# Loading 17 of 32 row pairs, and storing 11, as single 64 KB runs in a streaming softmax-gradient kernel

## The chip, the cores and the metric

The kernel runs on one core of a Trainium2 chip. The metric is the time of one execution on the device, in microseconds (us). A time with a range is the median of three to nine runs. The profiler adds nothing that matters: a profiled execution of the kernel before took 1248.14 us, the unprofiled ones 1248.03 to 1248.1 us.

## The reference, cut to what matters

```python
# logits: 8 x 1024 x 8192 float32, labels: 8 x 1024
logits_max = np.max(logits, axis=-1, keepdims=True)
exp_logits = np.exp(logits - logits_max)
softmax = exp_logits / np.sum(exp_logits, axis=-1, keepdims=True)
# one_hot has 1.0 at the label of each row
return (softmax - one_hot).astype(np.float32)
```

268 MB are read and 268 MB written, with a little arithmetic between: a streaming problem.

## The kernel before: the parts that matter

The 8192 rows are cut into 64 tiles of 128 rows (one per partition, 32 KB each). Tiles 2b and 2b+1 form block b: partition p holds rows 2p and 2p+1 of the block, which are neighbours in memory. Six slots of the on-chip buffer X hold one tile each. Here "row" means such a row tile, 4 MB.

```python
x_b = x_nv.rearrange("(b p j) v -> b p j v", p=P, j=G)   # G = 2
X = const.tile([P, SLOTS, V], fp32)                      # SLOTS = 6
...
def load(t, n):        # issued by SyncE; waits until the slot's old row is stored
    free = [stored[u - SLOTS] for u in range(t, t + n) if u - SLOTS in stored]
    w = run(nc.sync, free, got[t % SLOTS], "dma_start", out=sbuf(t, n), in_=hbm(x_b, t, n))
def store(t, n):       # issued by ScalarE; waits for the last arithmetic on the row
    w = run(nc.scalar, [finished[t + n - 1]], put[t % SLOTS], "dma_start", ...)
...
for t in range(T):     # cut to its order
    # ScalarE: x = exp(x - max), sum      VectorE: 1 / sum
    load(t + 1, 1)     # VectorE: maximum of row t + 1
    store(t - 1, 1)
    # ScalarE: x * 1/sum                  VectorE: subtract the one-hot row
```

## Time and profile before

| | before |
|---|---|
| time, median of 3 (range) | 1248.08 us (1248.03 to 1248.1) |
| bytes moved, mean rate | 536.98 MB, 431 GB/s |
| VectorE (DVE) busy, ScalarE (ACT) busy | 90%, 74% |
| last load landed, last store issued | 1199.2 us, 1229.6 us |

These lines of the page give the busy share of the DMA engines and the rate in 40 equal slices of the span, then the packets (here 16384 records of 32 KB, one for each run of bytes, and 2064 of 4 bytes, 16 for each of the 129 transfers, which I take for the semaphore writes), then the transfers with their median time from issue to landing.

```profile
DMA  9999999999999999999999999999999999999998
GB/s 406 418 430 433 435 434 430 433 435 433 431 434 434 433 431 434 434 432 431 434 435 432 431 434 434 431 433 434 435 431 433 433 434 432 432 433 435 431 432 385
DMA packets 18484, 536.98 MB, mean 431 GB/s; under 512 B 2064, under 2 KB 2064, under 8 KB 2096
...
X<-in_logits_dram SPq DMA_DIRECT2D x64, 4096.0 KB, 24.2
out_dram<-X ACTq DMA_DIRECT2D x64, 4096.0 KB, 55.1
```

The DMA is full in every slice but the last, and all from the third to the last but one read 430 to 435 GB/s. (A slice counts a packet whole where it starts, so single slices of the page after the change read up to 442.) A store needs 55 us from issue to landing and one is issued every 19.4 us, so two to three stores stand in their queue. The next lines are the view by stretches (start and end, length, busy time of PE, PEld, DVE, ACT and POOL with instruction counts, clock, DMA share, GB/s).

```profile
60.00:300.00 240.00, 0.00 (x0) 0.00 (x0) 240.00 (x43) 198.35 (x43) 0.00 (x0) 1.00 1.00 433
300.00:600.00 300.00, 0.00 (x0) 0.00 (x0) 269.80 (x48) 223.74 (x48) 0.00 (x0) 1.00 1.00 433
600.00:900.00 300.00, 0.00 (x0) 0.00 (x0) 270.78 (x47) 221.40 (x47) 0.00 (x0) 1.00 1.00 433
900.00:1050.00 150.00, 0.00 (x0) 0.00 (x0) 134.15 (x24) 111.95 (x24) 0.00 (x0) 1.00 1.00 433
```

The rate is 433 GB/s throughout. The end of the kernel in the timeline (start, length, engine, operation, tiles, and in brackets the idle time before it and what ended that):

```profile
1199.19 8.69 DVE L64 TENSOR_REDUCE m<-X 128x1 f32<-128x8192 f32 x1 [1.94 <-DMA X<-in_logits_dram]
...
1216.57 0.34 ACTq L64 DMA_DIRECT2D out_dram<-X  x1
...
1229.60 0.34 ACTq L64 DMA_DIRECT2D out_dram<-X  x1
```

The last load lands at 1199.2 us, and the last store is issued 30 us later. The stores that still stand in the queue fill those 30 us (426 to 439 GB/s in every 5 us from 1200 to 1230).

### The profile page before, as it was taken

Reading aid. Unit: us, or ns where it says so; the run is one execution under the profiler, and the core shown is the slowest. Engines: PE = TensorE matmul, PEld = TensorE weight load, DVE = VectorE, ACT = ScalarE, POOL = GpSimd, SP = SyncE. Lnnn points to the kernel's source line nnn. Section 1 sums busy time; section 2 is a strip of 40 time slices with the busy share of each in tenths; the row PEclk is TensorE's granted clock in tenths of the full one; section 3 lists DMA queues with packets and bytes.
Section 4 is the critical chain, followed back from the end, with each engine's and each line's share of the span. In section 5 each row is a group of like instructions: output and inputs, shape, how many; then the busy total and the mean of one; then the engine's idle time right before and its main releaser. Section 6 shows DMA issues by size and latency. Waiting matters only on the chain.

```text
span 1246.4 us, 592 instructions
## 1 busy us (share of the span) xinstructions
PE 0.4 (0%) x2; PEld 0.3 (0%) x2; DVE 1121.3 (90%) x196; ACT 919.0 (74%) x194; POOL 7.4 (1%) x7
## 2 busy tenths in 40 slices
PE   0000000000000000000000000000000000000000
PEld 0000000000000000000000000000000000000000
DVE  5999999999988989889898898998988989889893
ACT  3888888888767777677767777777777777677772
POOL 2000000000000000000000000000000000000000
DMA  9999999999999999999999999999999999999998
GB/s 406 418 430 433 435 434 430 433 435 433 431 434 434 433 431 434 434 432 431 434 435 432 431 434 434 431 433 434 435 431 433 433 434 432 432 433 435 431 432 385
DMA packets 18484, 536.98 MB, mean 431 GB/s; under 512 B 2064, under 2 KB 2064, under 8 KB 2096
## 3 DMA queue, kind: packets, MB, share of 16 engines
q1 hardware_dynamic: 9216, 268.44, 50.0%
q10 hardware_dynamic: 9264, 268.51, 49.9%
q14 instruction: 4, 0.03, 0.0%
HBM read 268.50 MB, written 268.44 MB: 431 GB/s over the span
## 4 chain that ended last, share of the span: by engine, by line
another core or an unknown queue 69%; DVE 21%; DMA 6%; SPq 1%; ACT 1%; DVEq 0%; issue 0%; PE 0%; ACTq 0%
DVE m L64 10%; DVE X L64 10%; DMA out_dram<-X 4%; DMA X<-in_logits_dram 2%; SPq L64 1%; ACT X L64 1%; DVE iota L64 0%; DVEq L52 0%; DMA lab_raw<-in_labels_dram 0%; DVE lab_f L64 0%; DVE r L64 0%; PE iota L64 0%; ACTq L64 0%; DVE lab L64 0%
## 5 line engine op out<-in xcount | busy, mean ns | idle before, releaser
L64 DVE TENSOR_REDUCE m<-X 128x1 f32<-128x8192 f32 x64 | 555.6, 8681 | 91.4 <-DMA X<-in_logits_dram 91.4
L64 ACT ACTIVATE X<-X,m 128x8192 f32<-128x8192 f32 x64 | 455.8, 7122 | 187.9 <-DVE m L64 187.9
L64 DVE SCALAR_TENSOR_TENSOR X<-iota,lab,X 128x8192 f32<-128x8192 int16 (+1 forms) x65 | 559.6, 8610 | 4.1 <-ACT X L64 4.1
L64 ACT ACTIVATE X<-X,r 128x8192 f32<-128x8192 f32 (+1 forms) x65 | 456.0, 7016 | 116.0 <-DVE r L64 116.0
L64 DVE RECIPROCAL r<-s 128x1 f32<-128x1 f32 x64 | 9.8, 153 | 7.3 <-ACT X L64 7.3
L64 ACT ACTIVATION_READ_ACCUMULATOR X<-X,m 128x1 f32 x64 | 11.9, 186 | 0.0
L64 DVE CAST lab_f<-lab_raw 32x256 f32<-32x256 int32 x1 | 3.5, 3526 | 4.9 <-DMA lab_raw<-in_labels_dram 4.9
L64 POOL IOTA X<- 128x8192 int16 x1 | 6.9, 6943 | 0.0
L64 DVE TENSOR_SCALAR iota<-X 128x4096 int32<-128x4096 int32 x1 | 4.4, 4427 | 0.1
L64 ACT ACT_TABLE_LOAD x1 | 1.3, 1283 | 1.4 <-SPq L52 1.4
L64 DVE COPY lab<-iota 128x64 f32<-128x64 f32 x1 | 0.2, 224 | 0.5 <-PE iota L64 0.5
L64 PE MATMUL iota<-ident,lab_f 32*128 32x32 f32 x2 | 0.4, 300 | 8.5 <-DVE lab_f L64 8.5
L64 PEld LDWEIGHTS iota<-ident,lab_f 32*128 32x128 f32 x2 | 0.3, 196 | 8.4 <-DVE lab_f L64 8.4
L64 POOL TENSOR_SCALAR_AFFINE_SELECT ident<-ident 32x32 f32<-32x32 f32 x1 | 0.2, 202 | 0.1
L64 POOL MEMSET ident<- 32x32 f32 x1 | 0.1, 114 | 0.5 <-SPq L52 0.5
L176 POOL MEMSET const-bfloat16-1.0<- 128x1 bf16 x1 | 0.1, 106 | 0.0
L176 POOL MEMSET const-uint8-127<- 128x1 uint8 x1 | 0.1, 106 | 0.0
L176 POOL MEMSET const-float32-0.0<- 128x1 f32 x1 | 0.1, 103 | 0.2 <-issue 0.2
L176 POOL MEMSET const-float32-1.0<- 128x1 f32 x1 | 0.1, 103 | 0.0
## 6 DMA issues: line engine op xcount, KB each, us to landing
X<-in_logits_dram SPq DMA_DIRECT2D x64, 4096.0 KB, 24.2
out_dram<-X ACTq DMA_DIRECT2D x64, 4096.0 KB, 55.1
lab_raw<-in_labels_dram ACTq DMA_DIRECT2D x1, 64.0 KB, 3.9
```

Of the source, the lines that this page charges most:

```text
L64: instruction = getattr(engine, method)(**operands)
L176: nc = _bacc.Bacc("TRN2", target_bir_lowering=False, num_devices=1)
```

## The change

The intent is to spend less on each run of bytes: where a block's two rows are loaded or stored together, each partition moves one run of 64 KB instead of two of 32 KB. Loads are paired in 17 of 32 blocks, stores in 11, the ends stay row by row, and the last load comes in two halves so that its maximum can start early.

```diff
+PAIRED_LOADS = (1, 2, 4, 5, 7, 8, 10, 11, 13, 14, 16, 17, 19, 20, 22, 23, 26)
+PAIRED_STORES = (4, 7, 10, 13, 16, 19, 22, 24, 26, 29, 30)
-        def load(t, n):
+        def load(t):
+            if t % G and t // G in PAIRED_LOADS:
+                return
+            n = G if t // G in PAIRED_LOADS else 1
             free = [stored[u - SLOTS] for u in range(t, t + n) if u - SLOTS in stored]
+            cols = halves if t == T - 1 else [slice(None)]
+            # one dma_start for each of cols
-        def store(t, n):
+        def store(t):
+            if t // G in PAIRED_STORES:
+                if t % G == 0:
+                    return            # the first row waits for the second
+                t -= t % G
+            n = G if t // G in PAIRED_STORES else 1
             w = run(nc.scalar, [finished[t + n - 1]], ...)
 ... (row_max of the last row: two halves and a minimum of the two)
```

More of the change, by code (lines that the diff above doesn't have):

```diff
@@ L47 @@
     m, s, r = (const.tile([P, T], fp32, name=n) for n in ("m", "s", "r"))
+    m_halves = const.tile([P, 2], fp32)
     iota = psum.tile([P, V], i16)
@@ L53 @@
         sem = tc.alloc_semaphore
-        got = [sem(f"got{i}") for i in range(SLOTS)]
+        got = [sem(f"got{i}") for i in range(SLOTS + 1)]
         put = [sem(f"put{i}") for i in range(SLOTS)]
@@ L100 @@
         loaded, stored, w_max, finished = {}, {-1: w_iota}, [], []
+        halves = [slice(0, V // 2), slice(V // 2, V)]
         def hbm(rows, t, n):
@@ L107, in sbuf @@
             return X[:, t % SLOTS : t % SLOTS + n, :]
-        def load(t, n):
+        def load(t):
+            if t % G and t // G in PAIRED_LOADS:
+                return
+            n = G if t // G in PAIRED_LOADS else 1
             free = [stored[u - SLOTS] for u in range(t, t + n) if u - SLOTS in stored]
-            w = run(nc.sync, free, got[t % SLOTS], "dma_start", out=sbuf(t, n), in_=hbm(x_b, t, n))
-            loaded.update(dict.fromkeys(range(t, t + n), w))
-        def store(t, n):
+            to, of = sbuf(t, n), hbm(x_b, t, n)
+            cols = halves if t == T - 1 else [slice(None)]
+            w = [
+                run(nc.sync, free, got[q], "dma_start", out=to[:, :, c], in_=of[:, :, c])
+                for q, c in zip((t % SLOTS, SLOTS), cols)
+            ]
+            loaded.update(dict.fromkeys(range(t, t + n), w))
+        def store(t):
[4 more added lines that the diff above has]
+            n = G if t // G in PAIRED_STORES else 1
             w = run(
@@ L121, in row_max @@
         def row_max(t):
-            w_max.append(run(
-                nc.vector, [loaded[t]], dve, "tensor_reduce",
-                out=m[:, t : t + 1], in_=X[:, t % SLOTS, :], axis=mybir.AxisListType.X, op=Alu.max, negate=True,
-            ))
-        load(0, 1)
+            x, to = X[:, t % SLOTS, :], m[:, t : t + 1]
+            parts = [(x, to)] if len(loaded[t]) == 1 else [(x[:, c], m_halves[:, i : i + 1]) for i, c in enumerate(halves)]
+            for arrived, (part, extreme) in zip(loaded[t], parts):
+                w = run(
+                    nc.vector, [arrived], dve, "tensor_reduce",
+                    out=extreme, in_=part, axis=mybir.AxisListType.X, op=Alu.max, negate=True,
+                )
+            if len(parts) == 2:
+                w = run(
+                    nc.vector, [w], dve, "tensor_tensor",
+                    out=to, in0=m_halves[:, 0:1], in1=m_halves[:, 1:2], op=Alu.min,
+                )
+            w_max.append(w)
+        load(0)
         row_max(0)
@@ L137 @@
             if t + 1 < T:
-                load(t + 1, 1)
+                load(t + 1)
                 row_max(t + 1)
             if t > 0:
-                store(t - 1, 1)
-            n = 1 if t + 1 < T else 2
-            cols = [slice(i * V // n, (i + 1) * V // n) for i in range(n)]
+                store(t - 1)
+            cols = [slice(0, V)] if t + 1 < T else halves
             scaled = [
@@ L158 @@
             finished.append(w)
-        store(T - 1, 1)
+        store(T - 1)
         for w in dict.fromkeys(stored[t] for t in range(T - SLOTS, T)):
```

## The prediction

> **What bounds the kernel now.** The DMA engines. The page shows 536.98 MB in a span of 1246.4 us, 431 GB/s, DMA at nine or more tenths in 39 of 40 slices; DVE is busy 90%, ACT 74%. The stretch views show DMA full from 2 to 1240 us. In steady state one row tile (4 MB in, 4 MB out) takes 19.35 us: the spacing of landings of successive stores; at the end, with stores alone, 9.675 us. [...] the trace's slices reach 435. [...]
>
> **What the change removes.** 17 pairs of loads and 11 pairs of stores become one transfer each. If a 64 KB run is one descriptor, each pair saves eight descriptors and one semaphore write on each engine[...]. A gain of 2% (25 us) is out of reach, since the bytes stay.
>
> **What it moves.** A paired load waits until both slots are stored, and its first row is usable only when both have landed; a paired store waits for its second row, about 19 us more. Slots have slack for it: a store takes 55 us from issue to landing (page, DMA issues), mostly queueing. Stepping the schedule through with the trace's durations (maximum 8.69, exponential with its read 7.3, scaling 7.12, last step 8.74, issue to first packet 1.4 us), the queues never run dry in the middle; pairing everything would idle the DMA by 90 us. DVE has 19.35 - 17.6 = 1.8 us of slack per row.
>
> The danger is the end. Before, DMA stays full to 1240 us: the last load lands at 1199.2, the last store is issued at 1229.6, while the store before it lands only at 1235.4. After, a paired store of rows 60 and 61 is issued later and the last load depends on how the engines share. [...] If a 64 KB packet counts as one turn, the late loads wait behind the 64 KB stores (the last one, in 16 KB halves of a row's 32 KB, gets a fifth of the engine), and DMA idles some 5 to 8 us near 1205 us: total about 1253. If shares stay equal by bytes, or the runs are cut into 32 KB, the end idles about 1 to 1.5 us: total 1247.5 to 1249.5. The list looks tuned, so I lean to the second.
>
> **Prediction.** 1248 us; 8 in 10 between 1245 and 1253. Faster by over 2%: 1%; within 2%: 97%; slower by over 2%: 2%.
>
> **What would show it.** Packets fall from 18484 by about 4000 if 64 KB goes as one. Steady spacing per pair of rows 38.7 us[...]. DMA slices stay at 9 to the last two or three, where one may dip. DVE waits for loads become fewer and longer. The last load's second half lands at 1190 to 1202.
>
> **What would make it wrong.** A 64 KB run handled faster or slower than two of 32 KB; a dry queue in the middle, repeated every three blocks; the packet turns starving the last loads more than I assume.

The sum came to 1248 us: the 1248.1 us before, less a small saving on packets, plus the 1 to 1.5 us of idle time at the end in the favoured branch (5 to 8 us in the other, hence its 1253). The eight and the one on each engine are in the trace before: a 4 MB transfer leaves 128 records of 32 KB and 16 of 4 bytes on 16 engines. The stepped schedule and the idle times are estimates from the durations listed there, and the two branches for how the engines share were suppositions.

## The result, and the profile after

| | before | after |
|---|---|---|
| time, median of 6 (range) | 1248.07 us (1247.91 to 1248.1) | 1260.38 us (1256.36 to 1262.96) |
| ratio | | 1.0096 (95%: 1.0076 to 1.0116) |

A ratio is the mean time of one kernel's fast runs over that of the other's of the same rounds, so it is not quite the ratio of the medians quoted. Executions over 1.5% slower than the fastest of the same kernel are left out of the means. The change costs about 1%, outside the predicted 1245 to 1253 us, and the time now varies by 6.6 us where it had varied by 0.2.

The same lines of the page, after:

```profile
DMA  9999999999999999999999999999999999999998
GB/s 402 426 433 441 426 439 425 434 434 432 430 427 442 421 422 433 432 422 434 423 434 414 437 427 428 415 428 438 420 413 433 417 426 432 434 433 432 438 428 367
DMA packets 14597, 536.98 MB, mean 427 GB/s; under 512 B 1633, under 2 KB 1633, under 8 KB 1665
...
out_dram<-X ACTq DMA_DIRECT2D x42, 4096.0 KB, 32.3
X<-in_logits_dram SPq DMA_DIRECT2D x29, 4096.0 KB, 26.6
X<-in_logits_dram SPq DMA_DIRECT2D x2, 2048.0 KB, 39.7
X<-in_logits_dram SPq DMA_DIRECT2D x17, 33.3
out_dram<-X ACTq DMA_DIRECT2D x11, 28.5
```

There are 3887 fewer packets, so a 64 KB run is one packet (the trace has 3584 records of 64 KB, 128 for each of the 28 paired transfers). The DMA share has not moved at all. The rate has: slices of 413 to 423 GB/s now come at intervals. A store lands 28 to 32 us after issue instead of 55: its queue has lost its backlog. By stretches:

```profile
60.00:300.00 240.00, 0.00 (x0) 0.00 (x0) 223.81 (x40) 184.82 (x40) 0.00 (x0) 1.00 1.00 433
300.00:600.00 300.00, 0.00 (x0) 0.00 (x0) 270.56 (x48) 223.59 (x48) 0.00 (x0) 1.00 1.00 429
600.00:900.00 300.00, 0.00 (x0) 0.00 (x0) 257.93 (x46) 217.78 (x46) 0.00 (x0) 1.00 1.00 428
900.00:1050.00 150.00, 0.00 (x0) 0.00 (x0) 133.35 (x23) 106.06 (x23) 0.00 (x0) 1.00 1.00 422
```

The engines are counted as busy all the time (share 1.00), but they deliver 1 to 2.5% less in the middle. 300 us at 429 instead of 433 are 2.8 us lost, the next 300 us at 428 are 3.5, and 150 us at 422 are 3.8: together about 10 us of the 11.6 by which the profiled run (1259.74 us) is longer. The loss is in the middle, and it is no idle time.

**Where it happens.** The timeline around one of the slow places:

```profile
414.00 8.74 DVE L68 SCALAR_TENSOR_TENSOR X<-iota,lab,X 128x8192 f32<-128x8192 int16 x1
...
426.64 8.69 DVE L68 TENSOR_REDUCE m<-X 128x1 f32<-128x8192 f32 x1 [3.82 <-DMA X<-in_logits_dram]
435.24 8.74 DVE L68 SCALAR_TENSOR_TENSOR X<-iota,lab,X 128x8192 f32<-128x8192 int16 x1
...
444.02 0.34 ACTq L68 DMA_DIRECT2D out_dram<-X  x1
```

Row 20 is finished at 422.7 us (414.00 + 8.74), but its store waits for row 21, finished at 444.0. Between 405.5 and 444.0 us no store is issued. The store before has landed by 438.1 us, and the trace's packet records show no store packet on any engine from 436.6 to 448.3 us: the store queue is dry and the engines run loads alone. When the paired store then arrives, this is what one of the 16 engines does (packet records of the trace; one engine's packets are told apart by each starting where the one before ends):

```
load   32 KB  443.12 -> 444.33   1.21 us
load   32 KB  444.33 -> 445.55   1.21
load   32 KB  445.54 -> 447.32   1.78   stretched
load   32 KB  447.32 -> 449.67   2.35   stretched
store  64 KB  449.66 -> 452.08   2.42
load   32 KB  452.08 -> 453.29   1.21
store  64 KB  453.29 -> 455.71   2.42
```

From about 445.4 us, 1.4 us after the store's issue (the first load's first packet started 1.4 us after its issue, at 2.38 us in the trace before), the last load packets before it take up to twice their time. An undisturbed packet takes 611 ns for 16 KB, 1213 for 32 KB and 2418 for 64 KB, the medians of the trace. I call what a packet takes beyond its size's median, where it is over 30 ns, "stretch", and sum it over all packets and divide by 16 engines. It is 1.3 us before and 12.0 us after. After the first 60 us there are ten stretches of time of over 10 us without a store packet. The table gives them with the packet stretch around the end of each (from 9 us before it to 6 us after):

| store queue dry, us | 203-214 | 319-331 | 437-448 | 554-565 | 672-683 | 790-802 | 908-920 | 977-989 | 1058-1074 | 1173-1184 |
|---|---|---|---|---|---|---|---|---|---|---|
| stretch, us | 0.2 | 0.8 | 1.0 | 1.3 | 1.7 | 1.5 | 1.7 | 1.5 | 0 | 0 |

Together 9.6 us. So the first theory, R: pairing a store makes it wait, the store queue runs dry, and when it starts again beside a running load the engines lose about a microsecond, some eight times. (The load queue runs dry as well, 18 times for 9 to 19 us after the first 60 us, with at most 0.1 us of stretch around the end of each. So it takes more than a dry queue to cost time.)

### The profile page after: what moved, and what is told of

The parts are those of the page before. It is cut to its first block, busy times and chain, and to the rows that moved or that the text cites. A ratio compares the mean times of both kernels' runs of the same rounds, so it can differ in the third digit from the quotient of the medians.

```text
span 1258.0 us, 575 instructions
## 1 busy us (share of the span) xinstructions
PE 0.4 (0%) x2; PEld 0.3 (0%) x2; DVE 1118.7 (89%) x198; ACT 919.0 (73%) x194; POOL 7.4 (1%) x7
## 4 chain that ended last, share of the span: by engine, by line
DVE 50%; DMA 48%; ACT 1%; DVEq 0%; issue 0%; PE 0%; ACTq 0%; SPq 0%
DMA X<-in_logits_dram 25%; DVE X L68 24%; DVE m L68 24%; DMA out_dram<-X 22%; ACT X L68 1%; DVE m_halves L68 1%; DVE iota L68 0%; DVEq L56 0%; DMA lab_raw<-in_labels_dram 0%; DVE lab_f L68 0%; DVE r L68 0%; PE iota L68 0%; ACTq L68 0%; DVE lab L68 0%; ACTq L214 0%
## 5 line engine op out<-in xcount | busy, mean ns | idle before, releaser
L68 DVE TENSOR_REDUCE m<-X 128x1 f32<-128x8192 f32 x63 | 546.4, 8673 | 110.1 <-DMA X<-in_logits_dram 110.1
L68 DVE TENSOR_REDUCE m_halves<-X 128x1 f32<-128x4096 f32 x2 | 8.7, 4406 | 0.0
```

The lines of the kernel that those rows point to most:

```text
L68: instruction = getattr(engine, method)(**operands)
```

## The experiments

All results were correct. The kernels are variants of the changed one; "before" was run beside each set and had medians of 1248.09 to 1248.14 us. The diffs are shortened.

### First set: which part costs

Loads alone.

```diff
-PAIRED_STORES = (4, 7, 10, 13, 16, 19, 22, 24, 26, 29, 30)
+PAIRED_STORES = ()
```

> All 17 paired loads and the split last load stay, every store goes row by row. Theory R (the loss comes when the store queue runs dry and starts again beside a running load, about 1.2 us a time, nine times, and about 3 us at the end): no store waits for its partner, the store queue never runs dry after the first 50 us, so 1246.5 to 1248.5 us and load packets stretched by no more than before (1.7 us per engine in sum). Rival S (64 KB load packets are themselves slower, or starve the stores by taking two turns' worth): half or more of the 12 us stays, 1253 us or more.

Measured: 1251.47 us (1249.99 to 1252.1), ratio 1.0029. No dry stretch after the first 52 us, stretch 2.0 us (before's, given as 1.7 in the expectation, is 1.3 by the definition above). The view by stretches is back to the kernel before:

```profile
300.00:600.00 300.00, 0.00 (x0) 0.00 (x0) 271.24 (x48) 224.27 (x48) 0.00 (x0) 1.00 1.00 433
600.00:900.00 300.00, 0.00 (x0) 0.00 (x0) 264.69 (x47) 218.30 (x47) 0.00 (x0) 1.00 1.00 434
900.00:1050.00 150.00, 0.00 (x0) 0.00 (x0) 137.28 (x25) 113.38 (x25) 0.00 (x0) 1.00 1.00 433
```

Paired loads cost nothing in the middle; rival S falls. About 3 us more than expected remain, taken up in the second set.

Stores alone: `PAIRED_LOADS = ()` and the last load whole.

> The 11 paired stores stay, every load goes row by row. Theory R: paired stores still wait for their second row and the store queue runs dry, some 5 to 8 times, the end also idles; 1252 to 1262 us. Rival S (the paired loads cost it): back to 1247 to 1249 us.

Measured: 1266.27 us (1261.84 to 1271.82), ratio 1.0148: above both ranges and worse than the whole change. Rival S falls again, but R does not explain it all. The store queue runs dry nine times with at most 0.4 us of stretch each; the 12.4 us of stretch lie elsewhere, half of them on store packets, and the engines drift apart (one transfer's landings on the 16 engines are spread over up to 29 us, where before it was 2.3). 11 us more idle time than before lie at the end: the last load lands only at 1225.3 us, with few stores left to fill the time.

The wait without the 64 KB store run: a "paired" store is issued as two 32 KB-run transfers, both when the second row is done.

```diff
-            w = run(nc.scalar, [finished[t + n - 1]], put[t % SLOTS], "dma_start",
-                    out=hbm(o_b, t, n), in_=sbuf(t, n))
+            for u in range(t, t + n):
+                stored[u] = run(nc.scalar, [finished[t + n - 1]], put[u % SLOTS], "dma_start",
+                                out=hbm(o_b, u, 1), in_=sbuf(u, 1))
```

> As after, but a paired store is issued as two transfers of 32 KB runs, both only when the second row is finished: the wait stays, the 64 KB store run goes. Theory R: the dry stretches of the store queue stay in the middle (about eight of 11 to 12 us from the last packet to the next), so about 1 us each is still lost; with a shorter end than after: 1254 to 1260 us. Rival U (the large packet of the restarting store is what stalls the engine, not the restart): 1247 to 1250 us, with stretched load packets at or below 3 us per engine in sum.

Measured: 1259.37 us (1257.4 to 1265.27), ratio 1.0098, as the whole change; stretch 8.1 us in the profiled run. It differs from the loads-alone kernel only in when eleven stores are issued. So the wait costs, and a long store packet is not needed; rival U falls.

Seven pairs, no pairs at the end: `PAIRED_STORES = (4, 7, 10, 13, 16, 19, 22)`.

> As after, but the last four paired stores (blocks 24, 26, 29, 30) go row by row. Theory R: the seven or eight dry stretches up to 920 us stay and cost 8 to 10 us, the end is full again: 1255 to 1258 us. Rival T (all of the loss is the end, the stretched packets cost nothing on balance): 1246 to 1249 us.

Measured: 1260.15 us (1254.92 to 1262.51), ratio 1.0091. Seven dry stretches, stretch 12.6 us. The list's odd tail is not the cause; rival T falls.

### Second set: the end, the dose, the size

Loads alone with the last load whole (`cols = [slice(None)]`).

> Paired loads only, and the last load in one piece again. The theory for the 2 to 4 us that the loads-only kernel still lost: the two 16 KB halves of the last load get a third of the engine against 32 KB stores, so it landed late and the last store was issued at 1235.7 instead of 1229.6 us. Then this kernel is back at 1246.5 to 1248.5 us, with the last store issued by 1231 us. Rival (paired loads cost something in the middle): it stays at 1250 to 1252 us.

Measured: 1247.93 us (1247.46 to 1248.47) against 1248.09, ratio 0.9999 (0.9986 to 1.0011). So the halves, not the pairs, cost the loads-alone kernel its 3 us (without the pairs they cost 1.2, as the run after next shows).

Three pairs: `PAIRED_STORES = (7, 13, 19)`, the rest as changed.

> As after with paired stores in blocks 7, 13 and 19 alone (seven of them and no tail gave 1254.9 to 1262.5 us, none gave 1250.0 to 1252.1 us). Theory R: three dry stretches of the store queue, near 320, 550 and 790 us, each 1 to 1.8 us of stretched load packets: 1253 to 1257 us. Rival (a paired store costs only through a lasting drift that any one of them sets off): as much as with seven, 1258 us or more; or nothing, 1250 to 1252 us.

Measured: 1255.11 us (1253.0 to 1256.6), ratio 1.0051. The dose fits: none 1251.5, three 1255.1, seven 1260.2 us. In the profiled run (1256.6) the account is less tidy, though: 4.4 us of stretch and 4.7 us of idle time at the end beyond before's.

The halves alone: no pairs.

> The kernel before with the last load in halves and nothing else. If packets take turns whatever their size, the second half lands later than the whole did (1199.2 us) and the last store is issued later: 1248.5 to 1251 us. If turns go by bytes, 1247 to 1248.3 us.

Measured: 1249.27 us (1249.17 to 1251.15), ratio 1.0013. The end of its timeline:

```profile
1208.86 4.42 DVE L68 TENSOR_REDUCE m_halves<-X 128x1 f32<-128x4096 f32 x1 [7.32 <-DMA X<-in_logits_dram]
...
1235.19 0.34 ACTq L68 DMA_DIRECT2D out_dram<-X  x1
```

The second half lands at 1208.8 us where the whole load had landed at 1199.2, and the last store is issued at 1235.2 instead of 1229.6. Between 1199 and 1206 us its packet records hold 72 load packets of 16 KB and 61 store packets of 32 KB: packets of the two sizes are about as many, so the loads got 37% of the bytes there. I read this as turns of about one packet for each queue, whatever its size. The halving meant to start the maximum early made it late.

All of the change with runs of 32 KB: the two slots of a pair are put three slots apart, so a pair is still one transfer with the same waits.

```diff
-            return X[:, t % SLOTS : t % SLOTS + n, :]
+            i = t % SLOTS
+            at = i // G + (i % G) * (SLOTS // G)
+            return X[:, at : at + (n - 1) * (SLOTS // G) + 1 : SLOTS // G, :] if n > 1 else X[:, at : at + 1, :]
```

> All of the change, but the two slots of a pair lie apart in the on-chip buffer, so a pair is still one transfer with the same waits and every run is 32 KB (about 18,500 packets again). Theory R in its plain form (any restart of a dry store queue costs about 1 us, the size of a packet does not matter): stepping it through gives some 16 dry stretches, so 1258 us or more. Rival V (the loss needs 64 KB packets, as turns that favour one queue or as long packets): 1248 to 1251 us, most of it at the end.

Measured: 1256.58 us (1254.94 to 1257.64), ratio 1.0067, a little under the range of plain R and far above that of V. The cost does not need 64 KB packets. But the place is another one: seventeen dry stretches of the store queue ended with 0.3 us of stretch or less each, and most of the 9.1 us came in bursts of 0.3 to 1.6 us within 20 us after the load queue had been dry for about 20 us and was issued to again. R in its plain form, every restart costs a microsecond, is wrong.

### Third set: paired stores with and without a dry queue

Every second paired load only, `PAIRED_LOADS = (1, 4, 7, 10, 13, 16, 19, 22)`, the last load whole, three or seven paired stores; the three-store control with all paired loads; and the seven-store kernel with the buffer's pairs of slots turned by one place.

> Paired stores in blocks 7, 13 and 19 as in the run with three of them, but only every second of the paired loads (blocks 1, 4, ... 22) and the last load whole. Stepped through with the rule that each packet is one turn, the stores then keep a backlog and their queue never runs dry. Theory R: no dry stretch, no stretched packets, 1247 to 1249 us. Rival W (a paired store costs about 1.2 us wherever it stands): 1251 to 1253 us.

Measured: 1254.02 us (1253.13 to 1254.72), ratio 1.0047, above both ranges. The premise failed: the store queue did run dry, three times for 6 to 9 us, with 0, 1.8 and 1.7 us of stretch.

> The control of the run above: all paired loads, paired stores in blocks 7, 13 and 19, the last load whole. Theory R: three dry stretches of 11 to 12 us, 1 to 1.6 us of stretching each: 1250.5 to 1253.5 us. Rival W: the same time as the run above.

Measured: 1250.66 us (1249.71 to 1251.39), ratio 1.0022. Three dry stretches as expected, but only 0.0, 0.4 and 0.2 us of stretch at them: the time lies in R's range, and not for R's reason. Neither theory foresaw that this control would be the faster of the two.

> The run with seven paired stores and no paired tail, with the three pairs of slots in the on-chip buffer turned by one place, so that the restarting stores read another part of it. If the cost of a restart is a matter of timing between queues: 1255 to 1262 us as before. If it hangs on which part of the buffer the store reads (restarts near 1070 and 1180 us in the changed kernel, which read the last two slots, stretched nothing): 1250 to 1253 us.

Measured: 1259.84 us (1256.94 to 1262.07), ratio 1.0092. Which part of the buffer the store reads does not decide.

> Seven paired stores as in the run that had no paired tail, with every second paired load only and the last load whole. Stepped through there is no dry stretch in the middle, and about 3 us of idle time at the end. Theory R: 1248 to 1252 us against 1255 to 1262 us. Rival W (each paired store costs where it stands): 1255 us or more.

Measured: 1270.18 us (1268.94 to 1271.52), ratio 1.0177. The premise failed here too (seven dry stretches), and the end was far worse than stepped through: the last load landed at 1227.0 us, with 13.4 us more idle time than before. My reading, not tested: paired stores take 64 KB turns from single-row loads; the loads fall behind, and at the end no backlog of stores is left.

### Fourth set: feed the queue

The third set had left open whether paired stores cost as such. Here the first half of a pair's first row is stored as soon as that row is finished, and the other one and a half rows when the second is: 48 KB runs remain, the store queue is fed.

```diff
             if t // G in PAIRED_STORES:
-                if t % G == 0:
-                    return
+                lo, hi = (0, V // 2) if t % G == 0 else (V // 2, G * V)
+                # store columns lo to hi of the block when row t is finished
```

> All paired loads, the last load whole, and in the seven blocks with paired stores the first half of the first row is stored as soon as that row is finished (16 KB runs); the other one and a half rows go as 48 KB runs when the second row is finished. The large runs stay, but the store queue is fed again before it runs dry. Theory R: no dry stretch of 8 us or more in the middle, stretching within 2 us of before, 1246.5 to 1249.5 us. Rival W (large store runs, or waiting for the second row, cost where they stand): 1252 us or more.

Measured: 1248.07 us (1247.85 to 1248.74) against 1248.13, ratio 1.0000 (0.9986 to 1.0015).

> The control of the run above: the same seven blocks stored as true pairs, all paired loads, the last load whole. Theory R: seven dry stretches, 1252 to 1258 us, with 4 to 10 us of stretching. Rival W: within 1.5 us of the run above.

Measured: 1257.55 us (1255.26 to 1259.17), ratio 1.0069. First the fed kernel by stretches, then the control:

```profile
300.00:600.00 300.00, 0.00 (x0) 0.00 (x0) 271.04 (x48) 224.07 (x48) 0.00 (x0) 1.00 1.00 433
600.00:900.00 300.00, 0.00 (x0) 0.00 (x0) 263.47 (x47) 217.07 (x47) 0.00 (x0) 1.00 1.00 433
900.00:1050.00 150.00, 0.00 (x0) 0.00 (x0) 137.79 (x24) 114.25 (x24) 0.00 (x0) 1.00 1.00 434
```

```profile
300.00:600.00 300.00, 0.00 (x0) 0.00 (x0) 268.24 (x48) 221.26 (x48) 0.00 (x0) 1.00 1.00 427
600.00:900.00 300.00, 0.00 (x0) 0.00 (x0) 258.75 (x45) 217.60 (x46) 0.00 (x0) 1.00 1.00 425
900.00:1050.00 150.00, 0.00 (x0) 0.00 (x0) 135.61 (x23) 109.22 (x23) 0.00 (x0) 1.00 1.00 430
```

The fed kernel has no dry stretch after the first 52 us and 2.2 us of stretch; the control has seven, and 12.2 us. The two differ in nothing but how those seven stores are cut and when their first part is issued. Feeding the queue gives back all of the 9.4 us. So withholding the first row's store is shown to be the cause of the loss, twice: here, and in the held kernel against the loads-alone kernel (1259.4 against 1251.5 us), which differ in the time of issue alone. How the wait turns into lost time is less certain: 9.1 of the control's 12.2 us of stretch stand around its seven restarts of the dry store queue, but restarts after dry stretches as long cost next to nothing in the kernel with 32 KB runs.

### The account

For the profiled run of each kernel: the time beyond before's 1248.14 us, and from its packet records the change in stretch, in idle time of the engines up to the last packet, and in undisturbed packet time (medians times counts), each per engine.

| kernel | median, us | profiled: longer by | stretch | idle | packet time | sum |
|---|---|---|---|---|---|---|
| after | 1260.4 | +11.6 | +10.7 | +2.1 | -1.7 | +11.1 |
| loads alone | 1251.5 | +1.8 | +0.7 | +1.8 | -1.0 | +1.6 |
| loads alone, last whole | 1247.9 | -0.2 | +0.9 | -0.1 | -1.1 | -0.3 |
| stores alone | 1266.3 | +21.7 | +11.1 | +11.1 | -0.7 | +21.5 |
| held, 32 KB stores | 1259.4 | +9.7 | +6.8 | +3.6 | -1.0 | +9.4 |
| seven pairs, last whole | 1257.6 | +11.0 | +10.9 | +1.5 | -1.5 | +10.8 |
| the same, fed | 1248.1 | -0.1 | +0.9 | +0.0 | -1.0 | -0.1 |
| all with 32 KB runs | 1256.6 | +9.4 | +7.8 | +1.5 | +0.1 | +9.4 |
| half the loads, seven pairs | 1270.2 | +23.4 | +10.7 | +13.4 | -1.0 | +23.1 |

In these kernels stretch, idle time and saved packet time account for the difference to within half a microsecond or so. Busy and idle time fill the span, so the sum has to come out; the table says where the time went, not why.

## Why the prediction was wrong, point by point

- **The bound: right.** The DMA engines bound the kernel before and after (share 1.00 in every stretch above), and no variant won 2% (best ratio 0.9999).
- **The saving: right in kind.** A 64 KB run is one packet (3887 fewer; "about 4000" was predicted). It takes 2418 ns against twice 1213, so 8 ns are saved per run: 1.7 us in the account.
- **The sharing rule: the wrong branch was favoured.** The prediction named both and leaned to equal shares by bytes or runs cut to 32 KB. The traces show turns of about one packet, whatever its size: 64 KB store, 32 KB load, 64 KB store on the engine above; between 1190 and 1206 us of the changed kernel 74 load packets of 16 KB and 5 of 32 KB beside 92 store packets of 64 KB, so the loads got 19% of the bytes; and the half loads that came late in the halves-alone run (72 packets of 16 KB beside 61 of 32 KB). Every run was a packet record of its own: 256 of 16 KB, 9088 of 32 KB and 3584 of 64 KB make up the 536.87 MB of loads and stores. The list that "looks tuned" was no evidence.
- **The end, in that branch: mis-sized.** It foresaw 5 to 8 us of idle time near 1205 us. Measured were 2.1 us more idle time in all. The last half load landed at 1216.9 us, not at 1190 to 1202.
- **The step that failed: "the queues never run dry in the middle".** Its next words cost a dry queue as idle time of the engines alone, and these always had work: while the store queue was dry, loads ran. But the store queue alone was dry ten times for 11 to 16 us, because a paired store withholds a finished row for about 21 us and the backlog that would have bridged this is gone: a store took 55 us from issue to landing before, about 30 after. (It took 33.0 us with the loads paired alone, 33 to 35 with the stores paired alone and 23 to 25 with 32 KB runs throughout, so the 64 KB turns of one queue are not what empties it.) Around eight of the ten returns of the stores, running load packets were stretched, 9.6 us in all. The steady spacing, predicted as 38.7 us per pair of rows (less a small saving), became 39.2 (588.4 us for the 15 pairs between the dry stretches at 319.2 and 907.6 us). The sum of the prediction had no such term, though it had listed "a dry queue in the middle, repeated every three blocks" among what would make it wrong. The held kernel and the fed kernel, each with its control, show that the withheld row is the cause.
- **"DMA slices stay at 9": right, and useless.** A stretched packet counts as busy: the share is 1.00 at 422 GB/s as at 433. GB/s by slice or stretch would have been the thing to name.
- **VectorE's waits for loads: right.** Fewer and longer: 19 waits of 110.1 us in all, where 47 had taken 91.4 us (the view of waits). VectorE still has idle time to spare.

Open: why one restart costs 1.7 us and another nothing. Two restarts of the changed kernel, at 1074 and 1184 us, were free; so were nearly all store restarts of the kernel with 32 KB runs, which paid at load restarts. The length of the dry stretch, the size of the arriving packet, the part of the buffer read and the direction each fail to sort them; the load queue of the loads-alone kernel restarted 16 times after 9 to 12 us without packets, with 0.1 us of stretch or less each. Also open: the spread of 6.6 us between executions, since each kernel has one profile, and the drifting apart of the engines in the stores-alone run.

No variant beats the kernel before. Paired loads with the last load whole and the fed stores tie with it (ratios 0.9999 and 1.0000): the 1 us saved on packets (1.1 and 1.0 in the account) is met by as much stretch (0.9 and 0.9), within what these runs can tell.

## What to carry to other kernels

When the DMA engines are the limit, do not hold back a store that is ready in order to merge it with the next one without measuring: the wait can cost more than the merge saves, even though the engines never idle (here 9.4 us against less than 2). Where a run is one packet and each queue gets about one packet per turn, as here, run lengths set the shares (16 KB load runs beside 32 KB store runs got 37% of the bytes, and the last half load landed at 1208.8 us where the whole had landed at 1199.2), so making one side's runs longer or cutting the other's shorter can move bandwidth from one queue to the other and change what is left to do when the kernel ends. Judge a full DMA by its GB/s, not by its busy share (here 1.00 at 422 GB/s and at 433).
